# A down projection in pairs: the order in which a pair's left weights, its added rows and the later sums load, and where two low parts are subtracted

## The chip, the cores and the metric

The kernel runs on one core of a Trainium2 chip. The metric is the device time of one execution in microseconds, the median of several runs. Six kinds of engine work beside each other and are tied together by semaphores only: TensorE (PE in the profile, with its weight loads as PEld), VectorE (DVE), ScalarE (ACT), GpSimd (POOL), SyncE (SP), and 16 DMA engines that SP and POOL feed. Each engine carries out its own instructions strictly in the order in which they stand in its queue, so an instruction that waits holds up everything behind it.

## The reference

A trunk of two layers over 512 positions of 1024 channels in float32. Each layer is a token mixer and a gated feed-forward block, each with a residual:

```
u, v = split(rmsnorm(x, ffn_norm[l]) @ w_up[l])          # 1024 -> 2 x 2816
u    = causal_dwconv(u, ffn_conv_w[l], ffn_conv_b[l])
x    = x + (gelu(u) * v) @ w_down[l]                      # 2816 -> 1024, the part that matters here
```

The mixer of layer 0 is pooling and short convolution, that of layer 1 gated linear attention. The result is a last rmsnorm of x. All weights come from HBM once.

## The kernel before

**Float32 products.** A float32 operand is split into a high part, rounded to fp32r on ScalarE (`high`), and a low part, which VectorE gets by subtracting the high part from the source (`low`). A product is three passes of TensorE: high by high, high weights by low data, low weights by high data. So a weight tile is ready for its first two passes when ScalarE is done with it and for the third when VectorE is.

**The down projection.** The 2816 rows of w_down are 22 blocks of 128. Ten of them (`NPLAIN`) are multiplied plainly, in two halves of five blocks for each of the eight output tiles (`plain_down`, the products at line 274). The other twelve go through a seven-product scheme (Strassen's kind) that makes two output tiles at once: the left and the right halves of the rows, the left and the right output tile, the first and second 256 positions. There are four such pairs p = 0 to 3 in each layer (`down_seven`, products at line 611), each of seven products p1, p2, p6, p5, p7, p3, p4 in that order, with 18 matmuls each. The outputs of a pair go to tiles called stx, stz and dn in PSUM.

**The weights of a pair.** `seven_weights` brings the eight main blocks: s31 (a sum of three quarters: one load on SP at line 473, then an accumulating DMA on POOL at line 477), the left output tile's 512 KB (`load_left`, line 481) and half of the right one's (`load_right`, line 485). It makes the operands a1 (left), s31, S2 and S4 from them. `extra_weights` brings the four added row blocks: for pair 0 as in `seven_weights`, for the later pairs 384 KB (`load`, line 553, tile raw_e) and 128 KB (`load_right`, line 567, tile xe). Its `first_sums` and `sums` (lines 562 to 572) make the same sums, and its high and low parts are at lines 581 (ACT, hi_e) and 586 (DVE, lo_e). Of lo_e there are four subtractions in a pair: the whole left part (needed by p1), S2's left part, 256 wide (p6), the sums' part (p5), and the right part (p3).

**Order.** Each step is put into a list with a due time in microseconds (`at`), counted from the planned start of the pair's first product (`base`), and `run_plan` (line 447) sorts the list and emits it. On TensorE, VectorE and ScalarE that order is the order of the queue. SP and POOL are not in the planned set (line 444): a load there stands in its queue where it becomes free to go, which is when its buffer has been released, and of several loads that want a buffer of the same ring the one earlier in the list gets it. The ring that matters is `raw`, three buffers of 128x1024 (`wp`, line 89): a pair's left weights, its right weights, its added rows, and the blocks of the plain products between the pairs all take their turn in it. A left buffer comes free after `s4_sum` (line 512), one of added rows after the sums' low part (line 586), a right one after the last low part of a2 (line 501), a plain block's after its low part (line 233).

**Outputs.** `keep` (line 874, ACT) copies a half of a product's sum out of PSUM, since a later product of the pair goes on adding to the same bank: kk after p1 and p6 (p7 waits for the second), uu after p7 and p4 (p4 waits for the first). `free_left` (line 898) takes the left tile's sum together, `add_x` (lines 890 and 894, DVE) scales it by the norm and adds it to x, and `finish` squares x on ScalarE for the next norm; in layer 1 a second ScalarE instruction, at line 1571, scales x as well. The left tile of pair p is added to x while pair p+1 runs.

The times of one pair are those of the tuple `ET` (line 67, thirteen steps of `extra_weights`), of the tuple for the pool "dn" in `seven_weights` (line 529), and of `begin` in `down_seven` (line 855: sum's load, sum's add, left, right, all ahead of `base`).

Of the kernel before, what the change touches and what calls it, by code (L numbers as in the profile page):

```python
# [39 lines left out]
HK = KD // 2  # L40
# [23 lines left out]
DOWN_RIGHT = [NPLAIN + HK + i for i in range(HK)] + [NF - 2, NF - 1]  # L64
NDOWN = 4
MIXT = (19.6, 25.3, 31.0, 36.7, 42.4, 48.1)
ET = (-16.0, -11.5, -9.0, -3.2, -1.7, 0.0, 0.7, 2.2, 3.6, 2.4, 4.4, 5.3, 8.4)

COLS = {}
_n = 0  # L70
# [12 lines left out]
def trunk_kernel(ctx, tc, xT, cols, w_first, w_lead, w_ab, w_pool, w_abo, w_vg, w_qk, w_r, w_g2, w_go, w_up, w_dn, w_ds, w_de, out):  # L83
# [11 lines left out]
    def slot(dt=F32, name="s"):  # L95
        return big.tile([P, T], dt, tag="s", name=name)
# [86 lines left out]
    def f32(ap):  # L183
        return ap.bitcast(F32)
# [256 lines left out]
    def at(t, fn):  # L441
        events.append((t, len(events), fn))
# [98 lines left out]
    def extra_weights(src, base, queued):  # L541

        e = {}
        blocks = src.rearrange("p (a n) -> p a n", a=4)

        def load():
            raw = e["raw"] = wp.tile([P, WBLK], F32, tag="raw", name="raw_e")
            if queued:
                nc.sync.dma_start(raw[:, : 2 * EXTRA], src[:, : 2 * EXTRA])
                e["s31"] = raw[:, 2 * EXTRA :].rearrange("p (a n) -> p a n", a=2)  # L550
                nc.sync.dma_start(e["s31"], blocks[:, 2:3, :].broadcast_to([P, 2, EXTRA]))
            else:
                nc.sync.dma_start(raw[:, : 3 * EXTRA], src[:, : 3 * EXTRA])

        def queued_sum():
            if queued:
                G.dma_start(e["s31"], blocks[:, 0:4:3, :], accum_op=ALU.add)

        def first_sums():
            if not queued:  # L560
                r, c = e["raw"], slice(2 * EXTRA, 3 * EXTRA)
                V.tensor_tensor(r[:, 3 * EXTRA :], r[:, c], e["xe"][:, c], ALU.add)
                V.tensor_tensor(r[:, c], r[:, c], r[:, :EXTRA], ALU.add)

        def load_right():
            e["xe"] = stage["dn"].tile([P, 3 * EXTRA], F32, tag="xe", name="xe", bufs=1)
            nc.sync.dma_start(e["xe"][:, 2 * EXTRA :], src[:, 3 * EXTRA :])

        def sums():
            r, t = e["raw"], e["xe"]  # L570
            V.scalar_tensor_tensor(t[:, :EXTRA], r[:, 3 * EXTRA :], -1.0, r[:, :EXTRA], ALU.mult, ALU.subtract)
            V.tensor_tensor(t[:, EXTRA : 2 * EXTRA], r[:, EXTRA : 2 * EXTRA], t[:, :EXTRA], ALU.subtract)

        def part(kind, i, lo, hi):
            if (kind, i) not in e:
                e[kind, i] = wsp.tile([P, WPITCH], F32R, tag=kind, name=f"{kind}_e")[:, SKEW : SKEW + WBLK]
            return e[kind, i][:, lo:hi], e["xe" if i else "raw"][:, lo:hi]

        def high(*args):
            h, raw = part("hi", *args)  # L580
            S.activation(h, raw, AF.Copy)

        def low(*args):
            h = part("hi", *args)[0]
            low, raw = part("lo", *args)
            V.tensor_tensor(low, raw, f32(h), ALU.subtract)

        whole, sums_31, left, right = (0, 0, 2 * EXTRA), (0, 2 * EXTRA, WBLK), (1, 0, EXTRA), (1, EXTRA, 3 * EXTRA)
        for t, step in zip(ET, (
            load, queued_sum, load_right, lambda: high(*whole), lambda: low(*whole), first_sums, sums,  # L590
            lambda: high(*left), lambda: low(*left), lambda: high(*sums_31), lambda: low(*sums_31),
            lambda: high(*right), lambda: low(*right),
        )):
            at(base + t, step)
        return e

    def seven_product(w, b, ops, name, out, first, ts, only=None, low_last=False, extra=None):
        if out not in b:
            b[out] = bank("st" + out)
        piece, side = LEFT[name]  # L600
        ks = [slice(side * QUARTER + k * P, side * QUARTER + (k + 1) * P) for k in range(HK)]
        h, lo = [[t[:, c] for c in ks] for t in w[piece]]
        if extra:
            i, c = EXTRA_AT[piece]
            ks = [slice((c + side) * EXTRA + k * P, (c + side) * EXTRA + (k + 1) * P) for k in range(HD - HK)]
            h, lo = [x0 + [extra[e, i][:, c] for c in ks] for x0, e in ((h, "hi"), (lo, "lo"))]
        ah, al = ops[name]()
        for i in range(3) if only is None else (only,):
            wt, a = ((h, ah), (lo, ah), (h, al))[i] if low_last else ((h, ah), (h, al), (lo, ah))[i]
            for k in range(len(a)):  # L610
                PE.matmul(  # L611
                    b[out][:, ts], wt[k], a[k],
                    start=first and i == 0 and k == 0, stop=i == 2 and k == len(a) - 1,
                    skip_group_check=True,
                )
# [73 lines left out]
    def ffn(l, acc, mixed, finish, ahead, halves_last=False):  # L689
# [131 lines left out]
        base = 5 * UNIT  # L821
# [30 lines left out]
            )  # L852

        def down_seven(p, base):
            w = seven_weights(w_ds[l, p], base, "dn", 2, begin=(26.0, 20.0, 11.0, 6.2))
            extra = extra_weights(w_de[l, p], base, p == 0)
            b, q = {}, {}

            def product(name):
                if not ops:  # L860
                    for n in LEFT:
                        ops[n] = lambda n=n: [[mixed_m[n, i][e] for i in range(HD)] for e in range(2)]
                b["yz"] = o.get(2 * p)
                out, first, ts = {
                    "p1": ("x", True, lo_t), "p2": ("yz", False, lo_t), "p6": ("x", False, lo_t),
                    "p5": ("z", True, lo_t), "p7": ("x", False, lo_t), "p3": ("yz", False, hi_t),
                    "p4": ("x", False, lo_t),
                }[name]
                seven_product(w, b, ops, name, out, first, ts, extra=extra)

            def keep(tile, ts):
                if tile not in q:
                    q[tile] = slot(name=tile)
                S.activation(q[tile][:, ts], b["x"][:, lo_t], AF.Copy)

            def add_p5(tile):
                V.tensor_tensor(q[tile][:, hi_t], b["z"][:, lo_t], q[tile][:, hi_t], ALU.add)

            for n, name in enumerate(DOWN_SEVEN):
                at(base + n * DOWN_UNIT, lambda name=name: product(name))  # L880
            at(base + 1 * DOWN_UNIT + 0.1, lambda: keep("kk", lo_t))
            at(base + 3 * DOWN_UNIT + 0.1, lambda: keep("kk", hi_t))
            at(base + 4 * DOWN_UNIT + 0.2, lambda: add_p5("kk"))
            at(base + 5 * DOWN_UNIT + 0.1, lambda: keep("uu", hi_t))
            at(base + 5 * DOWN_UNIT + 0.6, lambda: add_p5("uu"))
            at(base + 7 * DOWN_UNIT + 0.1, lambda: keep("uu", lo_t))
            return q

        def add_x(j, out, ts=slice(0, T), queued=False):
            V.tensor_tensor(out, out, rs[:, ts], ALU.mult)  # L890
            if queued:
                G.dma_start(x[j], out, accum_op=ALU.add)
            else:
                V.tensor_tensor(x[j][:, ts], out, x[j][:, ts], ALU.add)  # L894

        def free_left(p):
            kk = parts[p]["kk"]
            V.tensor_tensor(kk, o[2 * p], kk, ALU.add)
# [12 lines left out]
        t = base + 9 * UNIT  # L911
        blocks = list(down_blocks())
        parts = {}
# [15 lines left out]
        def sevens(p):  # L929
            nonlocal t  # L930
            parts[p] = down_seven(p, t)
            t += 7 * DOWN_UNIT

        def done_left(p, then):
            at(t - 1.8, lambda: free_left(p))
            at(then + (1.9 if p < HK - 1 else -1.1), lambda: add_x(2 * p, parts[p]["kk"], queued=False))
            at(then + (4.0 if p < HK - 1 else 0.9), lambda: finish(2 * p))

        def done_right(p, t):
# [8 lines left out]
        for p, (j, n) in enumerate(order):  # L948
            sevens(p)
            gap = 1.5 * n * NPLAIN * MM if p < HK - 1 else 0.0  # L950
            done_left(p, t + gap)
            if p < HK - 1:
                done_right(p, t + gap + 4.9)
            elif halves_last:
                at(t + 0.5, lambda: early_right(p))
            else:
                for i in range(KD - 2):
                    at(t - 2.6 + 1.25 * i, lambda i=i: pre_split(i, "mix1"))
            plain_down(j, n)
# [18 lines left out]
    parts = {}  # L978
# [398 lines left out]
    t = 0.0  # L1377
# [353 lines left out]
```

## Time and profile before

| what | value |
|---|---|
| median of 3 runs | 1002.59 us (1002.36 to 1004.91) |
| the profiled execution's own time | 1000.72 us |
| its span | 999.0 us |
| PE busy | 986.5 us (99%) |
| DVE busy | 881.0 us (88%) |
| ACT busy | 622.1 us (62%) |
| POOL busy | 88.7 us (9%) |
| DMA | 155.22 MB, 155 GB/s in the mean |
| four down pairs of layer 0, from the first product | 390.33 us |
| four down pairs of layer 1, from the first product | 914.71 us |

Times in the views count from the start of the span. A timeline row has the start, the time from there to the end of the last instruction of the row, engine, line, operation, tiles (out<-in), the number of instructions, and in brackets how long the engine had been idle before and what ended that. A row of waits has who waited for whom, the microseconds in total, how many times, and the longest. On SP a row is the issuing of a DMA, not its transfer.

### The profile page before, as it was taken

The page shows a single profiled execution, that of the slowest core. Times are in us where ns is not written, and L with a number is a line of the kernel's source. Part 1 is how long each engine was busy: PE and PEld are TensorE (multiplying, and loading weights), DVE is VectorE, ACT ScalarE, POOL GpSimd, SP SyncE. Part 2 cuts the span into 40 slices and gives each one's busy share as a digit, 9 for nine tenths or more (in the row PEclk, how much of TensorE's full clock was granted, in tenths as well). Part 3 has the DMA queues.
Part 4 walks back from the last instruction along what each step waited for, and adds up shares of the span by engine and source line. Part 5 has one row for each costly group of instructions (what it writes and reads, how often), then busy time and mean ns, then how long its engine had stood idle before and what let it go on. Part 6 is the DMA issues. An engine that isn't in the chain of part 4 may idle for free. (4 is left out here: it accounts for less than half of the span.)

```text
span 999.0 us, 18588 instructions
## 1 busy us (share of the span) xinstructions
PE 986.5 (99%) x7324; PEld 932.7 (93%) x7324; DVE 881.0 (88%) x1368; ACT 622.1 (62%) x1035; POOL 88.7 (9%) x111
## 2 busy tenths in 40 slices
PE   9999999999999999999999999999999999999997
PEld 7888889999999988999999999899999999988997
DVE  7886689999999899798879789889999999899796
ACT  6432567766766665455876566667766666665553
POOL 0000111111101000002000000110110111000000
PEclk9999999999999999999999999999999999999999
DMA  7423847788788454627335453767788777454622
GB/s 253 141 86 106 193 113 172 212 209 199 182 210 186 123 139 121 159 80 198 101 104 141 116 119 115 198 150 172 210 211 196 187 208 186 116 145 123 157 86 93
DMA packets 69240, 155.22 MB, mean 155 GB/s; under 512 B 5824, under 2 KB 9280, under 8 KB 69152
## 3 DMA queue, kind: packets, MB, share of 16 engines
q1 hardware_dynamic: 50560, 119.03, 37.7%
q0 software_dynamic: 18304, 34.61, 21.0%
q8 instruction: 57, 0.93, 0.4%
q10 hardware_dynamic: 288, 0.40, 0.1%
q14 instruction: 31, 0.25, 0.1%
HBM read 149.29 MB, written 2.10 MB: 152 GB/s over the span
## 5 line engine op out<-in xcount | busy, mean ns | idle before, releaser
L495 ACT ACTIVATE hi<-raw 128x1024 fp32r<-128x1024 f32 x120 | 125.7, 1058 | 52.1 <-DMA raw<-in_w_ds 23.0
L501 DVE TENSOR_TENSOR lo<-raw,hi 128x1024 fp32r<-128x1024 f32 x120 | 146.2, 1219 | 11.4 <-ACT hi L495 11.1
L477 POOL DMA_DIRECT2D s<-in_w_up x44 | 53.3, 1211 | 474.4 <-DVE v L1087 95.6
L229 ACT ACTIVATE hi<-raw 128x1024 fp32r<-128x1024 f32 (+3 forms) x69 | 61.4, 891 | 28.3 <-PE px L274 9.1
L233 DVE TENSOR_TENSOR lo<-raw,hi 128x1024 fp32r<-128x1024 f32 (+3 forms) x69 | 70.2, 1020 | 6.8 <-ACT hi L229 6.2
L370 DVE SCALAR_TENSOR_TENSOR cacc<-u,colt,cacc 128x511 f32<-128x511 f32 x96 | 71.4, 744 | 2.6 <-ACT cacc L367 2.5
L501 DVE TENSOR_TENSOR lo<-s,hi 128x1024 fp32r<-128x1024 f32 x60 | 73.0, 1217 | 0.0
L367 ACT ACTIVATE cacc<-u,colt 128x512 f32<-128x512 f32 x48 | 39.2, 816 | 45.4 <-DVE u L733 41.8
L495 ACT ACTIVATE hi<-s 128x1024 fp32r<-128x1024 f32 x60 | 63.3, 1056 | 1.8 <-ACT sh L495 1.0
L611 PE MATMUL stx<-th,hi 128*128 128x256 f32 x416 | 64.4, 277 | 0.0
L611 PE MATMUL stx<-th,lo 128*128 128x256 f32 x416 | 64.1, 276 | 0.0
L611 PE MATMUL stx<-tl,hi 128*128 128x256 f32 x416 | 64.1, 276 | 0.0
L611 PE MATMUL styz<-xh,lo 128*128 128x256 f32 x400 | 61.8, 277 | 0.7 <-DVE lo L501 0.7
L611 PE MATMUL styz<-xh,hi 128*128 128x256 f32 x400 | 62.0, 277 | 0.0
L611 PE MATMUL styz<-xl,hi 128*128 128x256 f32 x400 | 61.6, 276 | 0.0
L611 PEld LDWEIGHTS stx<-th,hi 128*128 128x128 f32 x416 | 54.9, 188 | 0.4 <-ACT n L1445 0.2
L611 PEld LDWEIGHTS stx<-tl,hi 128*128 128x128 f32 x416 | 54.9, 188 | 0.0
L611 PEld LDWEIGHTS stx<-th,lo 128*128 128x128 f32 x416 | 54.9, 188 | 0.0
L611 PEld LDWEIGHTS styz<-xh,lo 128*128 128x128 f32 x400 | 52.8, 188 | 0.9 <-DVE lo L501 0.9
L611 PEld LDWEIGHTS styz<-xh,hi 128*128 128x128 f32 x400 | 52.9, 188 | 0.0
L611 PEld LDWEIGHTS styz<-xl,hi 128*128 128x128 f32 x400 | 52.8, 188 | 0.0
L495 ACT ACTIVATE sh<-raw 128x512 fp32r<-128x512 f32 x60 | 37.9, 632 | 22.5 <-DVE raw L506 22.5
(391 smaller groups left out, 2669.6 us busy)
## 6 DMA issues: line engine op xcount, KB each, us to landing
s<-in_w_up SPq DMA_DIRECT2D x44, 512.0 KB, 6.9
s<-in_w_up POOLq DMA_DIRECT2D x44, 512.0 KB, 7.1
raw<-in_w_up SPq DMA_DIRECT2D x44, 512.0 KB, 6.5
raw<-in_w_up SPq DMA_DIRECT2D x44, 256.0 KB, 3.4
raw<-in_w_dn SPq DMA_DIRECT2D x32, 320.0 KB, 2.9
raw<-in_w_ab SPq DMA_DIRECT2D x12, 512.0 KB, 3.8
raw<-in_w_abo SPq DMA_DIRECT2D x8, 512.0 KB, 3.5
s<-in_w_ds SPq DMA_DIRECT2D x8, 512.0 KB, 5.8
```

The lines of the kernel that those rows point to most:

```text
L229: S.activation(parts[0], raw, AF.Copy)
L233: V.tensor_tensor(parts[1], raw, f32(parts[0]), ALU.subtract)
L367: S.activation(acc[0], u, AF.Identity, bias=col(bname, j), scale=col(wname, 2 * nj + j))
L370: V.scalar_tensor_tensor(a, u[:, : T - i], col(wname, (2 - i) * nj + j), a, ALU.mult, ALU.add)
L477: G.dma_start(w["s31"].rearrange("p (a n) -> p a n", a=2), part, accum_op=ALU.add)
L495: S.activation(h, src(), AF.Copy)
L501: V.tensor_tensor(lo, src(), f32(h), ALU.subtract)
L611: PE.matmul(b[out][:, ts], wt[k], a[k], start=first and i == 0 and k == 0, stop=i == 2 and k == len(a) - 1, skip_group_check=True,)
```

## The change

Four places, all of them due times:

```diff
-ET = (-16.0, -11.5, -9.0, -3.2, -1.7, 0.0, 0.7, 2.2, 3.6, 2.4, 4.4, 5.3, 8.4)
+ET = (-16.0, -11.5, -9.0, -3.2, -1.7, 0.0, 0.7, 2.2, 2.25, 2.4, 4.4, 5.3, 7.6)
...
-        for t, step in zip(ET, (
+        for t, step in zip(ET if queued else (-10.6, *ET[1:]), (
...
-            w = seven_weights(w_ds[l, p], base, "dn", 2, begin=(26.0, 20.0, 11.0, 6.2))
+            w = seven_weights(w_ds[l, p], base, "dn", 2, begin=(23.5, 15.5, 11.0, 6.2))
...
-            at(then + (1.9 if p < HK - 1 else -1.1), lambda: add_x(2 * p, parts[p]["kk"], queued=False))
+            at(then + (2.3 if p < HK - 1 else -1.1), lambda: add_x(2 * p, parts[p]["kk"], queued=False))
```

- The added rows of pairs 1 to 3 load at -10.6 in place of -16.0, which is behind the same pair's left weights (-11.0) in place of ahead of them.
- The load of s31 moves from -26.0 to -23.5 and its add from -20.0 to -15.5.
- The low part of S2's added rows moves from 3.6 to 2.25, and the addition of the previous pair's left tile into x from 1.9 to 2.3, so that they change places on VectorE.
- The low part of the added right rows moves from 8.4 to 7.6, which is ahead of the p5 addition into kk (due 8.38, line 877).

Nothing is computed differently, and no instruction is added or taken away.

## The prediction

> **What bounds the kernel now.** The page comes first: TensorE is busy nearly throughout, so the time is its work plus its pauses, and a change of due times can only touch the pauses. The waits of PE come second, to see which pauses lie in the down pairs.
>
> ```profile
> span 999.0 us, 18588 instructions
> PE 986.5 (99%) x7324; PEld 932.7 (93%) x7324; DVE 881.0 (88%) x1368; ACT 622.1 (62%) x1035; POOL 88.7 (9%) x111
> PE stx L611 <- ACT uu L874: 1.8, 2, 1.0
> PE stx L611 <- DVE lo_e L586: 0.9, 3, 0.3
> PE stx L611 <- ACT kk L874: 0.2, 1, 0.2
> ```
>
> That is 2.9 us, all at tiles of the pairs. What it really costs is seen in TensorE's timeline, from the start of one pair to the next, since the first matmuls after a wait also run longer.
>
> ```profile
> 390.33 0.63 PE L611 MATMUL stx<-bh,hi 128*128 128x256 f32 x4
> 400.55 0.62 PE L611 MATMUL dn<-bh,hi 128*128 128x256 f32 x4
> 403.76 0.73 PE L611 MATMUL stx<-xh,hi 128*128 128x256 f32 x4 [1.01 <-ACT uu L874]
> 405.92 0.62 PE L611 MATMUL stx<-bh,hi 128*128 128x256 f32 x4
> 424.20 0.63 PE L611 MATMUL stx<-bh,hi 128*128 128x256 f32 x4
> 442.77 0.63 PE L611 MATMUL stx<-bh,hi 128*128 128x256 f32 x4
> ...
> 914.71 0.63 PE L611 MATMUL stx<-bh,hi 128*128 128x256 f32 x4
> 924.93 0.62 PE L611 MATMUL dn<-bh,hi 128*128 128x256 f32 x4
> 927.88 0.73 PE L611 MATMUL stx<-xh,hi 128*128 128x256 f32 x4 [0.75 <-ACT uu L874]
> 930.03 0.62 PE L611 MATMUL stx<-bh,hi 128*128 128x256 f32 x4
> 939.20 0.73 PE L611 MATMUL stx<-xh,hi 128*128 128x256 f32 x4 [0.24 <-ACT kk L874]
> 943.40 0.62 PE L611 MATMUL stx<-xh,hi 128*128 128x256 f32 x4
> 948.87 0.63 PE L611 MATMUL stx<-bh,hi 128*128 128x256 f32 x4
> 963.16 1.32 PE L274 MATMUL dn<-mh,hi 128*128 128x512 f32 x5
> 966.59 0.63 PE L611 MATMUL stx<-bh,hi 128*128 128x256 f32 x4
> ```
>
> The last three rows give a pair that waits for nothing (pair 2 of layer 1): 963.16 - 948.87 = 14.29 us for its seven products (2.04 each), and 966.59 - 948.87 = 17.72 with the plain block behind it. Against that, layer 0 loses 15.59 - 14.29 = 1.30 in pair 0, 18.28 - 17.72 = 0.56 in pair 1 and 18.57 - 17.72 = 0.85 in pair 2; layer 1 loses 15.32 - 14.29 = 1.03 in pair 0 and 18.84 - 17.72 = 1.12 in pair 1. **Together 4.86 us**: the most that this change can win here.
>
> Why does ScalarE come late with uu? Its timeline, SP's, and VectorE's rows that release the buffers:
>
> ```profile
> 402.38 1.06 ACT L495 ACTIVATE hi<-raw 128x1024 fp32r<-128x1024 f32 x1 [5.33 <-DMA raw<-in_w_ds]
> 403.35 0.36 ACT L874 ACTIVATE uu<-stx 128x256 f32<-128x256 f32 x1
> ...
> 392.59 0.69 DVE L512 TENSOR_TENSOR raw<-raw 128x512 f32<-128x512 f32 x1
> 395.46 0.69 DVE L586 TENSOR_TENSOR lo_e<-raw_e,hi_e 128x512 fp32r<-128x512 f32 x1
> ...
> 393.34 0.33 SPq L553 DMA_DIRECT2D raw_e<-in_w_de  x1
> 395.24 0.38 SPq L473 DMA_DIRECT2D s<-in_w_ds  x1
> 396.18 0.33 SPq L481 DMA_DIRECT2D raw<-in_w_ds  x1
> 412.85 0.33 SPq L553 DMA_DIRECT2D raw_e<-in_w_de  x1
> 416.04 0.33 SPq L481 DMA_DIRECT2D raw<-in_w_ds  x1
> ```
>
> The copy of uu (p7's sum, which p4 waits for) stands behind the high part of the next pair's left weights, and that had waited 5.33 us for its transfer. The left weights went out at 396.18, right after lo_e had ended at 396.15 and freed a buffer; the buffer freed before, at 393.28 by line 512, had gone at 393.34 to the added rows, which stand earlier in the list. Pair 2 repeats it (412.85, then 416.04).
>
> **The change part by part.** *Left weights ahead of added rows.* The two now swap buffers, so the left weights of pair 1 go out at 393.34 and the added rows at 396.18; no transfer is added, and the bytes in SP's queue up to this point are the same. How long do they take?
>
> ```profile
> raw<-in_w_ds SPq DMA_DIRECT2D x3, 512.0 KB, 5.8
> raw_e<-in_w_de SPq DMA_DIRECT2D x3, 384.0 KB, 3.0
> ...
> DMA to landing us min/median/max: 3.1/5.6/8.3
> ```
>
> The first two rows are the medians in the window 390 to 442; the third is over all loads of the main pair weights. At 5.8 the left weights land at 399.1, at the shortest at 396.4, at the longest at 401.6. p4 is due at 400.55 + 2.04 = 402.59. The copy of uu takes 0.36 and the high part ahead of it holds ScalarE for 403.35 - 402.38 = 0.97, so p4 starts unhindered if the weights land by about 401.2. I take 399.1: ScalarE has the high part done before p7's sum exists, and **the wait of p4 goes: 1.30 in layer 0, 1.03 in layer 1.** The same load in pairs 2 and 3 goes out 3.2 us sooner as well (416.04 - 412.85), besides what the pairs gain.
>
> What is late next? VectorE. After p3 of pair 0 its queue runs on without a pause in pair 1, and the first in it, line 898, needs p3's sum. Here are its rows and the copy of kk that p7 waits for, first in layer 0, then in layer 1:
>
> ```profile
> 405.22 0.68 DVE L898 TENSOR_TENSOR kk<-dn,kk 128x512 f32<-128x512 f32 x1
> 411.19 0.69 DVE L894 TENSOR_TENSOR xall<-kk,xall 128x512 f32<-128x512 f32 x1
> 411.80 0.42 DVE L586 TENSOR_TENSOR lo_e<-xe,hi_e 128x256 fp32r<-128x256 f32 x1
> 413.92 0.36 ACT L874 ACTIVATE kk<-stx 128x256 f32<-128x256 f32 x1
> ...
> 929.33 0.68 DVE L898 TENSOR_TENSOR kk<-dn,kk 128x512 f32<-128x512 f32 x1
> 935.30 0.69 DVE L894 TENSOR_TENSOR xall<-kk,xall 128x512 f32<-128x512 f32 x1
> 938.79 0.36 ACT L874 ACTIVATE kk<-stx 128x256 f32<-128x256 f32 x1
> 943.60 0.69 DVE L898 TENSOR_TENSOR kk<-dn,kk 128x512 f32<-128x512 f32 x1 [0.87 <-PE dn L611]
> ```
>
> In the last row line 898 starts 0.20 after TensorE has gone on from p3 to p4 (943.40). So in the changed kernel it can start at 402.59 + 0.20 = 402.8, and what stands ahead of it is done by then: it starts 405.22 - 403.71 = 1.51 after the copy of uu now, and that copy will end at about 402.59 - 2.04 + 0.20 + 0.36 = 401.1. That is 2.4 earlier than 405.22, while pair 1 itself starts at 404.63 in place of 405.92, only 1.3 earlier. VectorE wins 1.1 us on TensorE, and pair 1's wait for lo_e in p6 (0.56 in all) is covered by that alone. I count **0.56 and, in pair 2 of layer 0, where the left weights come 3.2 us sooner, 0.85 as gained.**
>
> *S2's low part ahead of the sum into x.* It takes 0.42 of VectorE's queue and is ready sooner by the two instructions of the addition (0.68 and 0.69), which p6 no longer needs; the addition into x comes 0.42 later, and behind it on ScalarE stand finish, a2's high part, the high part of the added right rows and the copy of kk. In layer 0 that copy ends 414.28 - 411.88 = 2.40 after the addition. From line 898 to the end of the addition are 6.66, so the addition ends at 402.8 + 6.66 + 0.42 = 409.9, the copy at 412.3, and p7 is due at 404.63 + 4 x 2.04 = 412.8: free. In layer 1 finish has a second instruction and the copy ends 939.15 - 935.99 = 3.16 after the addition. Line 898 starts at 924.93 + 2.04 + 0.20 = 927.17, the addition ends at 927.17 + 6.66 + 0.42 = 934.25, the copy at 937.41; p7 is due at 924.93 + 6 x 2.04 = 937.17. So **0.24 of waiting stays, with the slower restart (0.73 for 0.62) about 0.3**, of the 1.12 lost there now. Without this edit it would be gone: its price is 0.3, and it is worth nothing as long as VectorE stays ahead. Bounds: 0 to 0.5 lost.
>
> *The right rows' low part ahead of kk's p5 addition.* A subtraction of the width of lo_e (0.69 above) goes ahead of a shorter addition. It moves no wait for TensorE otherwise, since kk is next read at line 898, after p3. Nothing; at worst 0.3 in a layer.
>
> *The later sums.* Their load goes out when the s31 buffer is free (395.24, between two others), not at its due time, so SP's order should stay. If it moved behind the left weights, these would gain up to a transfer, which they no longer need, and the sum is wanted only by pair 2. Nothing either way.
>
> **The sum**: 4.86 - 0.3 = 4.55 us. The profiled execution took 1000.72 (span 999.0 and 1.72 around it), so 996.2 there; the median lies 1.87 above it, so **998.0** on the scale of the medians, 0.45% faster. Nothing behind the pairs takes it back: the buffers there are released by the same instructions, which come sooner by as much.
>
> **The rivals.** *A smaller gain.* With less than 1.1 us won by VectorE, because the left weights land later than 401.2 or its queue is held at the added rows' low part, p6 and p7 keep part of their waits in pairs 1. For it: VectorE runs pair 1 without a pause now. Against it: those waits are 0.56 and 1.12 in all. If both stay in full and only the two waits of p4 and the 0.85 go, the gain is 3.2; if half of p4's wait stays too, 2.0. Time 999.4 to 1000.6.
>
> *The added rows become late: slower.* They now go out last, and ScalarE, in order, waits for them ahead of S2's high part and the sums' (lines 495), VectorE behind that. In pair 1 they go out at 396.18 and VectorE wants their high part at 403.4 (line 898 and 0.6), so they have until 402.7: 6.5 us. In pair 3 I estimate about 6 too. Beyond that each microsecond costs one in each of three pairs of two layers, since VectorE's queue has no pause there. The turning point is 6 x (d - 6.3) = 4.55, d = 7.1 us. Their row says 3.0; against it, they now follow 512 KB in the same queue, and the longest of the neighbouring loads took 8.3. At 8.3 it would be 12.0 lost, 998.0 + 12.0 = 1010. The Trainium skill, "DMA: Bandwidth & Descriptors", section "Issuing engines are not separate DMA queues", speaks for this rival: transfers issued from different engines run on the same 16 DMA engines and interleave, so POOL's accumulating sum of the next pair takes its share too. By that rule the added rows of pair 2 might take twice their 3.0, 6 us, still inside the room; no row here shows the two side by side in the new order.
>
> *It doesn't do what it says.* If SP's order doesn't follow the list, only VectorE's reordering is left, and the 0.42 in front of the addition lengthens p7's wait in layer 1: 0.56 gained, 0.42 lost, about 1002.4. Against it: the rows at 393.34 and 412.85 follow the list.
>
> **How the numbers follow.** Forecast (gain over 3 us) 0.72; smaller gain 0.13; added rows late 0.10, of which 0.08 slower; order not followed 0.05. What a measurement of this kernel can tell from no change is about 0.3%, 3 us. So faster 0.72, within 0.3% 0.19, slower 0.09. The forecast's own range is 996.6 (all 4.86, and a median 1.1 lower, the runs before lying 0.2 to 2.3 from theirs) to 999.6; the range on record reaches over the smaller gain to 1001.5, and leaves out the late rows.
>
> **What would show it.** In SP's timeline: line 481 at the place of line 553 in pairs 1 to 3. In ScalarE's: no wait of microseconds for raw<-in_w_ds, and uu copied right after p7. In PE's waits: no uu and no lo_e, a little kk. Pair to pair: 14.3, 17.7, 17.7 in both layers, about 18.0 in pair 1 of layer 1. Wrong would be: hi_e (line 581) waiting for raw_e<-in_w_de, p5 or p7 of pair 3 waiting, or line 553 still ahead of line 481.

## The result and the profile after

The changed kernel took 996.93 us in the median of 6 runs (996.35 to 997.40), the kernel before 1002.98 us beside it (6 runs, 1000.89 to 1004.91). The ratio is 0.9939, with a 95% interval of 0.9926 to 0.9952: **0.6% faster**. The prediction was 998.0 us and 0.45%. The profiled execution of the changed kernel took 997.34 us with a span of 995.6, at a granted clock of 0.999.

First the page of the changed kernel, its span and busy times:

```profile
span 995.6 us, 18579 instructions
PE 985.7 (99%) x7324; PEld 932.5 (94%) x7324; DVE 881.2 (89%) x1368; ACT 622.5 (63%) x1035; POOL 89.0 (9%) x111
```

The engines carry out as many working instructions as before; the 9 by which the first line differs from the 18588 of the kernel before are among those that none of these rows counts. TensorE is busy for 0.8 us less with the same matmuls: the first four after a wait take 0.73 us in place of 0.62, and there are fewer waits. Then the waits of PE in the changed kernel (who waited for whom, microseconds in total, times, longest):

```profile
PE warm L170 <- DVE half L176: 1.1, 1, 1.1
PE pu L1001 <- ACT xh L995: 1.0, 2, 0.5
PE styz L611 <- DVE lo L501: 0.7, 1, 0.7
PE vg L1209 <- DVE z L1157: 0.2, 1, 0.2
```

The three rows at tile stx that had 2.9 us in the kernel before (for uu, lo_e and kk) are gone, and nothing in the down pairs has come in their place (styz is no tile of theirs, and the kernel before has the same row of 0.7). The start of the products in TensorE's timeline gives the cost in full:

```profile
391.74 0.63 PE L611 MATMUL stx<-bh,hi 128*128 128x256 f32 x4
...
406.04 0.62 PE L611 MATMUL stx<-bh,hi 128*128 128x256 f32 x4
423.74 0.63 PE L611 MATMUL stx<-bh,hi 128*128 128x256 f32 x4
441.46 0.63 PE L611 MATMUL stx<-bh,hi 128*128 128x256 f32 x4
...
913.16 0.63 PE L611 MATMUL stx<-bh,hi 128*128 128x256 f32 x4
927.46 0.62 PE L611 MATMUL stx<-bh,hi 128*128 128x256 f32 x4
...
935.84 0.72 PE L611 MATMUL stx<-xh,hi 128*128 128x256 f32 x4
...
945.50 0.63 PE L611 MATMUL stx<-bh,hi 128*128 128x256 f32 x4
963.22 0.63 PE L611 MATMUL stx<-bh,hi 128*128 128x256 f32 x4
```

From one pair to the next these are 14.30, 17.70 and 17.72 us in layer 0 (before: 15.59, 18.28, 18.57) and 14.30, 18.04 and 17.72 in layer 1 (before: 15.32, 18.84, 17.72). Together 99.78 for 104.32: **4.54 us come out of the pairs**, where the prediction has 4.55. (These six stretches hold pairs 0 to 2 of each layer; pair 3, behind the last start, has no wait for a copy or a low part in either kernel.) What is left is the row at 935.84, p7 of pair 1 in layer 1.

SP's timeline shows the swap (each row is the issuing of one DMA):

```profile
394.74 0.33 SPq L481 DMA_DIRECT2D raw<-in_w_ds  x1
396.64 0.38 SPq L473 DMA_DIRECT2D s<-in_w_ds  x1
397.58 0.33 SPq L553 DMA_DIRECT2D raw_e<-in_w_de  x1
...
411.84 0.33 SPq L481 DMA_DIRECT2D raw<-in_w_ds  x1
...
415.03 0.33 SPq L553 DMA_DIRECT2D raw_e<-in_w_de  x1
```

Line 481, the left weights, goes first now, and line 553, the added rows, takes the place 2.84 us later (394.74 and 397.58); in pair 2 they change places in the same way, 3.19 us apart. Counted from the first product (391.74), the left weights leave 3.0 after it; before, it was 396.18 - 390.33 = 5.85 after it. In ScalarE's timeline of the same stretch, the wait of 5.33 us for that transfer is gone:

```profile
401.25 1.06 ACT L495 ACTIVATE hi<-raw 128x1024 fp32r<-128x1024 f32 x1 [2.79 <-PE stx L611]
402.22 0.36 ACT L874 ACTIVATE uu<-stx 128x256 f32<-128x256 f32 x1
402.95 0.63 ACT L581 ACTIVATE hi_e<-raw_e 128x512 fp32r<-128x512 f32 x1 [0.37 <-DMA raw_e<-in_w_de]
```

The high part now waits for TensorE. It runs to 402.31, a little past the end of p7 (p3 begins at 401.96), and the copy of uu behind it is done at 402.58, 1.4 us ahead of p4 (2.04 after the start of p3). The third row is the new edge: the high part of the added rows waits for its own transfer, by 0.37 us, which nothing has to pay for yet.

### The profile page after: what moved, and what is told of

Read it like the earlier page. It is cut to its first block, busy times and chain, and to the rows that moved or that the text cites. A ratio compares the mean times of both kernels' runs of the same rounds, so it can differ in the third digit from the quotient of the medians.

```text
span 995.6 us, 18579 instructions
## 1 busy us (share of the span) xinstructions
PE 985.7 (99%) x7324; PEld 932.5 (94%) x7324; DVE 881.2 (89%) x1368; ACT 622.5 (63%) x1035; POOL 89.0 (9%) x111
## 4 chain that ended last, share of the span: by engine, by line
PE 95%; DVE 2%; DMA 1%; ACT 0%; issue 0%; SPq 0%; DVEq 0%; ACTq 0%
PE stx L611 34%; PE styz L611 19%; PE dn L274 11%; PE go L274 4%; PE abo L274 4%; PE dn L611 3%; PE stz L611 2%; PE pc L274 2%; PE pb L274 2%; PE px L274 2%; PE pu L1001 2%; PE vg L1209 2%; PE vg L1211 2%; PE vg L1210 1%; DMA raw_lead<-in_w_lead 1%; PE o L1300 1%
```

## The experiments

The theory was that of the prediction: the left weights' place in SP's order is all that counts, through ScalarE's queue (uu for p4) and through VectorE's (lo_e for p6). The rivals were that VectorE's new order or the sums' new due times bring part of it, that uu's place behind the high part is the whole cause, and that the added rows are paid for by their later place. All kernels below compute the same as the two kernels. Times are compared with runs of the kernel before beside them. These took 1001.34 us (23 runs, 999.16 to 1002.67) for the load alone, VectorE's order alone, the same from the other side and the sums' due times alone, and 1001.71 us (22 runs, 1000.57 to 1004.24) for the other four with several runs.

**The load's place alone**, on the kernel before:

```diff
-        for t, step in zip(ET, (
+        for t, step in zip(ET if queued else (-10.6, *ET[1:]), (
```

> Before, with only the added rows' load moved behind the left weights (-10.6 in place of -16.0 for pairs 1 to 3). Theory: this alone wins everything, since VectorE, no longer held by the left weights, gains 1.1 us on TensorE in pair 1 and so covers the waits for lo_e too. Pair to pair 14.3, 17.7, 17.7 in both layers, also in pair 1 of layer 1 (17.7, not 18.0, since the addition into x keeps its old place); 4.8 us less than before in the pairs of the profile, PE waiting for no uu, lo_e or kk. Rival: the waits are separate, the load edit wins only the two waits of p4 (1.30 and 1.03) and lo_e still holds p6 in pair 1 (18.1 to 18.3) of both layers: 2.3 us less.

Measured: 996.32 us (5 runs, 995.55 to 997.21), ratio 0.9954 (0.9942 to 0.9966). PE's waits in its profile have no row at a tile of the pairs:

```profile
PE warm L170 <- DVE half L176: 1.1, 1, 1.1
PE pu L1001 <- ACT xh L995: 0.7, 1, 0.7
PE styz L611 <- DVE lo L501: 0.7, 1, 0.7
PE vg L1209 <- DVE z L1157: 0.2, 1, 0.2
```

The pairs take 14.29, 17.71 and 17.72 us in both layers, 99.44 in all: 4.88 less than before. One due time carries the whole gain, the waits for lo_e and kk among it, though no instruction of VectorE or ScalarE was moved in the list.

**VectorE's new order alone**, on the kernel before:

```diff
-ET = (-16.0, -11.5, -9.0, -3.2, -1.7, 0.0, 0.7, 2.2, 3.6, 2.4, 4.4, 5.3, 8.4)
+ET = (-16.0, -11.5, -9.0, -3.2, -1.7, 0.0, 0.7, 2.2, 2.25, 2.4, 4.4, 5.3, 7.6)
...
-            at(then + (1.9 if p < HK - 1 else -1.1), lambda: add_x(...))
+            at(then + (2.3 if p < HK - 1 else -1.1), lambda: add_x(...))
```

> Before, with only the edits on VectorE's order (S2's low part 2.25, right rows' low part 7.6, addition into x 2.3); the loads stay as in before. Theory: p4 of pair 0 waits as before (pair 0 at 15.6 and 15.3), p6's wait of pair 1 in layer 0 goes (0.56), p7's in layer 1 grows by about 0.4, pair 2 of layer 0 loses a few tenths less; in all 0 to 1 us less than before, no difference that a measurement can tell. Rival: the low parts are half of what was won, 2.5 us less than before.

Measured: 1002.4 us (11 runs, 1001.12 to 1003.91), ratio 1.0013 (1.0004 to 1.0021), so about 1 us more, not less: a miss in the sign. The two waits of p4 stay and those for kk multiply, as TensorE's timeline of this kernel shows:

```profile
403.90 0.73 PE L611 MATMUL stx<-xh,hi 128*128 128x256 f32 x4 [0.87 <-ACT uu L874]
414.81 0.75 PE L611 MATMUL stx<-xh,hi 128*128 128x256 f32 x4 [0.44 <-ACT kk L874]
...
928.62 0.75 PE L611 MATMUL stx<-xh,hi 128*128 128x256 f32 x4 [1.29 <-ACT uu L874]
...
940.28 0.73 PE L611 MATMUL stx<-xh,hi 128*128 128x256 f32 x4 [1.16 <-ACT kk L874]
...
958.55 0.74 PE L611 MATMUL stx<-xh,hi 128*128 128x256 f32 x4 [0.28 <-ACT kk L874]
```

In the kernel before there was one wait for kk, of 0.24. Here there are three, 1.88 together. (The last of them, in pair 2 of layer 1, may be chance: another profile of the kernel before has a wait of 0.27 at that place.) The waits of p6 for lo_e are bought off (0.9 at stx in the kernel before, none here), but the addition into x comes later, and the copy of kk stands behind what follows the addition on ScalarE. The pairs take 105.89, 1.57 more than before. I had expected the two effects to be of one size and the first to win.

**The same from the other side**, the changed kernel with VectorE's order of S2's low part and the addition put back:

```diff
-ET = (..., 2.2, 2.25, 2.4, 4.4, 5.3, 7.6)
+ET = (..., 2.2, 3.6, 2.4, 4.4, 5.3, 7.6)
...
-            at(then + (2.3 if p < HK - 1 else -1.1), lambda: add_x(...))
+            at(then + (1.9 if p < HK - 1 else -1.1), lambda: add_x(...))
```

> The changed kernel, with S2's low part and the addition into x put back to their old places (3.6 and 1.9); the loads, the sums and the right rows' low part stay changed. Theory: the swap costs 0.3 us in pair 1 of layer 1 and wins nothing, so pair 1 of layer 1 takes 17.7 in place of 18.0 and the time is 0.3 us below that of the changed kernel, too little for a measurement (996.6 beside 996.9). Rival: the swap is what frees p6 from lo_e; p6 of pair 1 waits again in both layers, 0.5 to 1 us more than the changed kernel.

Measured: 995.94 us (5 runs, 995.43 to 996.38), ratio 0.9949 (0.9937 to 0.9961). Pair 1 of layer 1 takes 17.71 in place of 18.04, and all others are as in the changed kernel. So this edit costs 0.33 us there and brings nothing, while the right rows' low part at 7.6, which stays in, moves no pair. The time alone can't tell so small a difference. The same kernel ran once more, now beside the changed one:

> The changed kernel without the swap of S2's low part and the addition into x, once more, beside the changed kernel on the same chip. Theory: 0.3 us below the changed kernel by its profile (17.7 in place of 18.0 in pair 1 of layer 1), not told apart by the medians of 5 runs. Rival: 0.5 us or more below it.

It took 996.77 us (5 runs, 996.06 to 997.79), ratio 0.9951 (0.9937 to 0.9964), again with 17.71 in that pair.

> The changed kernel once more, on the chip of the others, to set beside them. Theory: its pairs are steady from run to run (14.3, 17.7, 17.7; 14.3, 18.0, 17.7), 4.5 to 5.0 us less than before by the medians; the 6.0 of the first comparison was 1 to 1.5 too much from the start of the kernel and from places outside the pairs, which vary between executions. Rival: the change also wins 1.5 us outside the pairs, 6 us less than before again.

The changed kernel beside it took 996.02 us (5 runs, 995.86 to 997.09), ratio 0.9942 (0.9930 to 0.9954), with 18.04. Its median lies 0.75 us below that of the kernel without the swap, where 0.3 above was expected, and the intervals overlap. The 0.33 us is a finding of the profiles (18.04 in all three profiles of the changed kernel, 17.71 in both without the swap and in the one with the load alone), not of the times. Against the kernel before, the changed one is 5.69 us faster here, more than the 4.5 to 5.0 expected; the part on the sum below comes back to it.

**The sums' due times alone**, on the kernel before:

```diff
-            w = seven_weights(w_ds[l, p], base, "dn", 2, begin=(26.0, 20.0, 11.0, 6.2))
+            w = seven_weights(w_ds[l, p], base, "dn", 2, begin=(23.5, 15.5, 11.0, 6.2))
```

> Before, with only the sums' due times moved (load -23.5, add -15.5). Theory: SP and POOL issue them when their buffer is free, so nothing moves: every queue's order is that of before, the ratio is 1.000 within 0.2%, and the profile is a second look at the program before: pairs at 15.6, 18.3, 18.6 and 15.3, 18.8, 17.7, if these waits are steady from run to run. Rival: the sums' loads make room for the left weights, about 1 us less than before, and the left weights land sooner after their issue. If the pairs of this second look are 1 to 2 us longer than in the first, the profile of before was a lucky execution and the waits vary with the transfers; this would explain that the medians differ by 6.0 where the pairs of the two profiles differ by 4.5.

Measured: 1001.52 us (12 runs, 1000.38 to 1003.03), ratio 1.0005 (0.9996 to 1.0013). Every queue's order in the pairs is that of the kernel before, the pairs take 104.28, and the waits at tile stx are much as before (view of PE's waits):

```profile
PE stx L611 <- ACT uu L874: 1.5, 2, 0.8
...
PE stx L611 <- DVE lo_e L586: 1.1, 3, 0.5
...
PE stx L611 <- ACT kk L874: 0.2, 1, 0.2
```

**p4's wait taken away without the load**: on the kernel before, the copy of uu is put ahead of the left weights' high part, by 0.3 of due time.

```diff
-            at(base + 5 * DOWN_UNIT + 0.1, lambda: keep("uu", hi_t))
+            at(base + 5 * DOWN_UNIT - 0.2, lambda: keep("uu", hi_t))
```

> Before, with only the copy of uu (after p7) put ahead of the high part of the next pair's left weights on ScalarE in pair 0: due at 5 units - 0.2 in place of + 0.1; all loads stay late. It takes the wait away without its cause. Theory (VectorE's lead on TensorE decides): p4 of pair 0 no longer waits (pair 0 at 14.3 in both layers, 1.30 and 1.03 less), but the left weights still land at the same time, VectorE gains less on them than TensorE does, and pair 1 gives part back: lo_e's wait in p6 grows by 0.3 to 0.7 (pair 1 at 18.6 to 19.0 in layer 0 and 19.2 to 19.6 in layer 1); about 1.3 us less than before in all, 0.1%. Rival: the wait itself was the loss; 2.3 us less than before, pair 1 unchanged at 18.3 and 18.8.

Measured: 1000.53 us (11 runs, 998.83 to 1002.48), ratio 0.9987 (0.9979 to 0.9996). Pair 0 becomes 14.30 and 14.29, as in the changed kernel, but pair 1 takes 18.61 and 19.37 and pair 2 of layer 1 takes 18.41. Of 2.32 us won in the two pairs 0, 1.55 are lost again in these three. Of these, the 0.86 of the two pairs 1 come from the edit: with the order of before they take 18.26 to 18.29 and 18.83 to 18.84 in all four profiles. The 0.69 of pair 2 may be chance, since one of those four has 18.35 there. With the 0.85 of pair 2 of layer 0, which had no wait here, the pairs gain 1.62 in all (102.70); that too happens in the kernel before by itself, as the last runs show. The timelines of ScalarE, VectorE and TensorE in this kernel say why:

```profile
400.83 0.39 ACT L874 ACTIVATE uu<-stx 128x256 f32<-128x256 f32 x1 [3.69 <-PE stx L611]
402.07 1.07 ACT L495 ACTIVATE hi<-raw 128x1024 fp32r<-128x1024 f32 x1 [0.86 <-DMA raw<-in_w_ds]
```

```profile
402.11 0.69 DVE L506 SCALAR_TENSOR_TENSOR raw<-s,raw 128x512 f32<-128x512 f32 x1 [2.23 <-DMA raw<-in_w_ds]
...
404.31 0.68 DVE L898 TENSOR_TENSOR kk<-dn,kk 128x512 f32<-128x512 f32 x1
```

```profile
411.36 0.51 PE L611 MATMUL stx<-eh,lo_e 128*128 128x256 f32 x2 [0.60 <-DVE lo_e L586]
...
933.84 0.50 PE L611 MATMUL stx<-eh,lo_e 128*128 128x256 f32 x2 [0.84 <-DVE lo_e L586]
```

uu is copied freely at 400.83, but VectorE sits for 2.23 us in front of the same transfer. It reaches line 898 at 404.31, 1.64 after p4's start (390.41 + 6 x 2.04 = 402.67, the first product of pair 0 being at 390.41); TensorE is early, VectorE isn't, and the difference comes out at lo_e. In the changed kernel line 898 starts 0.20 after p4's start:

```profile
404.20 0.69 DVE L898 TENSOR_TENSOR kk<-dn,kk 128x512 f32<-128x512 f32 x1
```

with p4 at 401.96 + 2.04 = 404.00. **Two engines waited for one transfer; only the earlier transfer frees both.**

**The added rows later still**: on the changed kernel, behind the right weights too.

```diff
-        for t, step in zip(ET if queued else (-10.6, *ET[1:]), (
+        for t, step in zip(ET if queued else (-6.0, *ET[1:]), (
```

> The changed kernel, with the added rows' load moved still further back, -6.0 in place of -10.6, behind the right weights and, in pairs 2 and 3, behind the buffer of the plain block: it goes out about 1 us later in pair 1 and about 2.3 us later in pairs 2 and 3. Theory of the prediction's slower rival: a room of about 6 us, beyond which each microsecond costs one. The rows took 5.3 us (median) in the changed kernel; with 1 to 2.3 us less room pair 1 still fits and pairs 2 and 3 wait for hi_e or lo_e by 0 to 1.5 us each in both layers, 0 to 4 us more than the changed kernel, my value 2. Rival: the rows' place costs nothing as long as the left weights are ahead; 997 as the changed kernel, pairs at 14.3, 17.7, 17.7.

Measured: 1000.9 us (12 runs, 998.68 to 1008.3), ratio 0.9996 (0.9980 to 1.0012), 4.9 us more than the changed kernel beside it. The pairs take 103.50 (3.72 more), with 19.64 and 19.39 in the pairs 2. SP's timeline shows the rows' load at the end of the group, and ScalarE's waits in the window 388 to 445 and TensorE's timeline show what waits for it:

```profile
410.64 0.33 SPq L481 DMA_DIRECT2D raw<-in_w_ds  x1
413.83 0.33 SPq L485 DMA_DIRECT2D raw<-in_w_ds  x1
...
416.10 0.33 SPq L553 DMA_DIRECT2D raw_e<-in_w_de  x1
```

```profile
ACT hi_e L581 <- DMA raw_e<-in_w_de: 6.6, 3, 3.3
```

```profile
423.42 0.50 PE L611 MATMUL stx<-bh,hi_e 128*128 128x256 f32 x2 [0.49 <-ACT hi_e L581]
431.86 0.50 PE L611 MATMUL stz<-eh,lo_e 128*128 128x256 f32 x2 [0.69 <-DVE lo_e L586]
```

In the changed kernel the same wait of hi_e is 0.4 us, once (0.7 and none in its other two profiles, 1.1 with the load alone). Here it is 6.6, and the wins of the left weights are all but gone. The late rows are a real price that the change comes close to and doesn't pay. I had put the cost at 2 us within 0 to 4; it was 3.7 in the pairs and 4.9 in the time.

**The swap in pair 1 alone**, on the kernel before (one execution; the edit also hands p to `extra_weights`, which is not shown):

```diff
-        for t, step in zip(ET, (
+        for t, step in zip((-10.6, *ET[1:]) if p == 1 else ET, (
```

> Before, with the left weights ahead of the added rows in pair 1 alone; pairs 2 and 3 load as before. Theory: pair 0 at 14.3 and pair 1 at 17.7 in both layers, and pair 2 of layer 0, whose left weights keep their late place but whose VectorE queue now starts 1 us sooner, keeps 0.2 to 0.8 of its 0.85 (17.9 to 18.5). Rival: pair 2 was late only because pair 1 was; 17.7.

Measured: 998.03 us. The pairs take 14.30, 17.70 and 18.21 in layer 0 and 14.30, 17.70 and 17.72 in layer 1. Pairs 0 and 1 are cured entirely, and pair 2 of layer 0 keeps 0.49 of its loss of 0.85. That would be the part that hangs on its own load; but that pair's loss varies by itself (next paragraph), so one profile doesn't settle how it divides.

**Three more executions of the two kernels**, to see how much of the profiles is chance:

> The kernel before, unchanged, one more look. Open: the medians of the two kernels differ by 5.7 to 6.0, the pairs of their profiles by 4.5. If the pairs of before lose 1 us more or less from execution to execution (the loss beside 99.74 was 4.6 in both looks so far), the rest lies in them; if they lose 4.3 to 4.9 again, it lies outside, in the start and in places that the edits don't touch.

> The kernel before, unchanged, a further look, for the same question: a loss of 4.3 to 4.9 us in the pairs again, or 5.5 and more.

> The changed kernel, unchanged, one more look. Its pairs at 14.3, 17.7, 17.7; 14.3, 18.0, 17.7 again. Its first pair started at 391.5 and 391.7 in the two looks so far, 1.1 to 1.4 after that of the others: by chance (390.3 to 391.7 this time), or by something in the program (391.4 to 391.8 again).

The kernel before took 1001.76 and 1000.31 us, with 104.58 and 103.36 in the pairs: pair 2 of layer 0 lost nothing in the second, and pair 2 of layer 1 lost 0.63 in the first. The changed kernel took 997.05, with 99.78 in the pairs, as in both earlier profiles of it, and its first pair began at 390.52.

## Why the prediction was right

**The place in SP's order: right, cause and size.** The left weights leave at the place of the added rows, the loss of p4 goes (1.30 and 1.03 predicted, 1.29 and 1.02 measured in the pairs 0), and with the load alone the kernel gains all of it. What the step had wrong are the two transfer times, and with them the moment at which ScalarE is done with the high part. It kept 5.8 us for the left weights and 3.0 for the added rows, from their rows in the old order. In the changed kernel, the view of the DMAs in the window 390 to 442 has:

```profile
raw<-in_w_ds SPq DMA_DIRECT2D x3, 512.0 KB, 3.3
raw_e<-in_w_de SPq DMA_DIRECT2D x3, 384.0 KB, 5.3
```

These are medians over three pairs, and the loads one by one (table in the last section) differ: in pair 1, on which p4 hangs, the left weights took 6.1 us before and 3.3 after, the added rows 3.0 before and 5.3 after. For the left weights the error lay on the safe side: they landed at 398.0, 3.2 us ahead of the high part, which then waited for TensorE and ended after p7 and not ahead of it, as the prediction had it. The copy of uu was in time all the same. For the rows the error ate the cover: of the 6.5 us that the prediction left them in pair 1, 5.3 are used here and 6.0 with the load alone, where it thought 3.0. That they still fit was luck as far as the row of 3.0 goes. The sentence from the Trainium skill that stood beside that rival ("DMA: Bandwidth & Descriptors", section "Issuing engines are not separate DMA queues"), by which the rows of pair 2 might take 6 us, was nearer: they took 5.6, 4.2 and 5.5 in the three profiles of the changed kernel, and in the first of them POOL's accumulating DMA went out at 413.99, shortly ahead of them. But the rows of pair 1 took 5.3 while POOL's next one went out only at 402.55, when they had all but landed; what was under way beside them were SP's own loads.

**VectorE wins 1.1 us on TensorE: right.** Line 898 starts 0.20 after p4's start where it started 405.22 - 403.76 = 1.46 after it: 1.26 won. The kernel with uu's copy moved is the counterproof: there p4's wait goes, but VectorE wins nothing (1.64 after p4's start), and pair 1's waits grow. The 0.56 and the 0.85 of layer 0 went, as counted. Of all terms the 0.85 is the least certain: one of three profiles of the kernel before had no wait in that pair, and its 18.21 with the swap in pair 1 alone leaves open how much its own load brings.

**S2's low part ahead of the addition: right.** Predicted 0.3 us in pair 1 of layer 1, measured 18.04 - 17.71 = 0.33. The working can be followed in the changed kernel, VectorE's timeline first, then ScalarE's:

```profile
925.62 0.69 DVE L898 TENSOR_TENSOR kk<-dn,kk 128x512 f32<-128x512 f32 x1
...
931.93 0.69 DVE L894 TENSOR_TENSOR xall<-kk,xall 128x512 f32<-128x512 f32 x1
```

```profile
935.43 0.36 ACT L874 ACTIVATE kk<-stx 128x256 f32<-128x256 f32 x1
```

From line 898 to the end of the addition are 932.62 - 925.62 = 7.00 us (predicted 6.66 + 0.42 = 7.08), from there to the end of the copy 935.79 - 932.62 = 3.17 (predicted 3.16). p7 was due at 935.62 and started at 935.84, and its first four matmuls took 0.72. No view names what released it; it starts 0.05 after the end of the copy, as it did in the kernel before, where the view does name the copy (939.15 and 939.20). With the load alone, where the addition stands as before, the copy comes early enough and the pair takes 17.71. That the edit is worth nothing "as long as VectorE stays ahead" held. But where VectorE isn't ahead it didn't pay either: alone, it lost about 1 us. The prediction's price for that case, 0.56 gained against 0.42 lost, was off in sign, since it saw one wait for kk and there were three, the largest 1.16 us.

**The right rows' low part and the sums' due times: right, nothing.** One is in the kernel with the swap undone, without a trace in any pair; the other alone changes neither an order nor the time (1.0005, 0.9996 to 1.0013).

**The sum and the scale.** The pairs gave 4.54 for 4.55. That it fits so closely is luck: counted from the other three profiles with the order of before, the same difference is 4.80, 3.58 and 4.50. The total is less exact still. The profiled execution was forecast at 996.2 and took 997.34, though the pairs agree, because its down pairs began 1.41 us later (391.74 for 390.33). In the other profiles of the changed kernel they began at 391.47 and 390.52, in those of the kernel before at 391.48 and 390.38, so this start varies in both kernels and is no part of the change. The medians on the other hand differ by more than the pairs do: 6.05 and 5.69 us for the changed kernel, 5.02 with the load alone, 5.40 and 4.94 with the swap undone, where the pairs of the profiles gained 4.54 and 4.88. **Between 0.1 and 1.5 us of the medians' difference isn't explained by these profiles.** The losses in the pairs of the kernel before vary by themselves (3.92 to 5.14 over the 99.44 of waitless pairs, in four profiles of its order, with that of the sums' due times), and so a median of the kernel before may hold more waiting than the profile from which I counted. That is only argued, since most of the timed executions have no profile. What the profiles do show is that the change wins nothing outside the pairs: the span without the six stretches is 894.7 to 895.5 us in the four profiles with the order of before and 895.5 to 895.8 in the three of the changed kernel.

**The rivals.** The smaller gain did not come, but the kernel with uu's copy moved shows what is left of the gain if the transfer is still late (ratio 0.9987). The late rows did not come, but came near, and did come when the load was put 4.6 later in the list. A fourth buffer for the ring, with which neither load would have to wait for the other, wasn't tried.

No kernel here beats the changed one beyond doubt. The load alone is the smallest edit, has 0.34 us less in its pairs, and can't be told from the whole change by its time.

## What to carry to other kernels

When an engine's wait ends with a transfer, look which load took the buffer that had come free before it: two loads that take turns in one ring can be swapped at no cost in bytes, and the one that more engines wait for belongs in front. Taking away the wait alone, by moving the instruction behind it, leaves the other engine that hangs on the same transfer, and part of the time comes back in the next pair. When two loads change places, don't keep the landing times that they had: look at what will be under way beside each in the new order, load by load and not by a median, and measure the room of the one put behind by moving it a step further.

## What the runs showed of the hardware that was not expected

Between two loads of one group, how long a transfer took went with its place, and not with its size, but only where other loads were under way beside them. The view of the DMAs, taken around each issue, has for layer 0 (time of issue, and us from there to landing):

| pair | kernel | first of the two | second of the two |
|---|---|---|---|
| 1 | before | added rows, 384 KB: 393.34, 3.0 | left weights, 512 KB: 396.18, 6.1 |
| 1 | changed | left weights: 394.74, 3.3 | added rows: 397.58, 5.3 |
| 2 | before | added rows: 412.85, 3.3 | left weights: 416.04, 5.8 |
| 2 | changed | left weights: 411.84, 4.1 | added rows: 415.03, 5.6 |
| 3 | before | added rows: 432.25, 3.0 | left weights: 435.41, 3.2 |
| 3 | changed | left weights: 430.59, 3.1 | added rows: 433.75, 3.1 |

In pair 1 the load of s31, another 512 KB, goes out between the two in both kernels (395.24 and 396.64) and is still under way when the second follows; from the first issue to the second landing it is 396.18 + 6.1 - 393.34 = 8.9 us before and 397.58 + 5.3 - 394.74 = 8.1 after. In pair 2 POOL's accumulating DMA goes out one microsecond ahead of the second load (415.04 and 413.99). In pair 3 no load of s31 goes out near them, the second load follows when the first has just landed, and both take about 3 us in either order. So the order decides who is served early, while the group as a whole takes about as long. That the other loads are the reason is argued from these rows; no run took one of them away.

The kernel with the late rows scatters more. With the rows at the end of the group, 12 runs spread over 9.6 us (998.68 to 1008.3); 11 runs with uu's copy moved, beside them, spread over 3.7 and 22 runs of the kernel before also over 3.7. Why isn't shown: one execution of it has a profile, and not one of the slowest.
